# A hybrid state-space and attention layer with another work sequence, another share for GpSimd, and p's first tokens loaded by themselves

## The chip, the core and the metric

The kernel runs on one core of one Trainium2 chip. The core has a matrix engine (TensorE, PE in the profile, with its weight loads as PEld), a vector engine (VectorE, DVE), an engine for activations (ScalarE, ACT), a general engine (GpSimd, POOL) and SyncE (SP), which issues the DMAs of this kernel. The engines work side by side, each through its own list of instructions, and wait for each other by semaphores. The metric is the device time of one execution in microseconds; the median of the runs counts.

## The reference

One layer for 1024 tokens of 1024 values. All is float32.

```python
x = layer_norm(x, ln_emb_g, ln_emb_b)
z = x @ w_in                                  # 1024 -> 1984
xs, gs, cq, ckv, kr, gm = split(z, 512, 512, 256, 128, 64, 512)
ys = s5_branch(xs, ...) * silu(gs)            # 32 groups of 16 channels, 64 complex states each,
                                              # linear recurrence over the tokens, GELU, sigmoid GLU
ym = mla_branch(cq, ckv, kr, ...) * silu(gm)  # 4 heads, RMS-normed latents, rotary part of 64,
                                              # causal softmax, 128 queries at a time
mix = concat(ys, ym) @ w_out                  # 1024 -> 1024
u = alpha * x + mix
out = layer_norm(u + sigmoid(u @ w_pg) * (p @ w_pp), ln_g, ln_b)
```

## The kernel before

**Precision.** A float32 product is made as three matmuls of a faster type: each operand is split into a high part (a cast) and a low part (a subtraction), and high·high, high·low and low·high are added up in PSUM (`mm3`, `split`). So each loaded weight tile costs one cast and one subtraction before TensorE may use it. In the names, an h or l at the end is the high or low part: wh and wl of a tile of w_in, yTh and yTl of an S5 output, pth and ptl of transposed softmax weights.

**Stages.** First p @ w_pp (tile pp, with p's and w_pp's parts in pr, ph, pl), kept in DRAM until the end. At the same time x is normalised and transposed (xt, xh, xl). Then the projection z in tiles of 128 columns by 512 tokens: xs first (the S5 input), then gm, the latents ("lat": cq, ckv, kr, gathered in Z) and gs. Beside it runs the S5 branch in four blocks b of 8 groups: matrices ("mats": mo, mt, bbh, bbl, transposed through TensorE into wt, kt, kb), input, state and output (y, sy, hu). Then the latents are normalised and transposed (cqh, krh, krl), `fold` multiplies the two up-projections of the query into wf (wfh, wfl), and `q_nope` and `q_rope` make the queries (qn, qr). Attention runs over 16 items, each a head and a pair of query blocks, in four stages one item apart: `scores` (s, masked p, softmax with rrec as 1/sum), `probs_t` (pt is the transposed p, pth and ptl its parts), `pv` (o, oh, ol) and `uv_out` (uv, gated into ymt and ymh). The GLU of the S5 output reads yT back from DRAM (`glu_y`), multiplies the S5 gate gsr by yT (`glu_gs` loads, `glu_yg` multiplies), makes glu tiles of 12 matmuls, and a sigmoid sg whose product is ysh and ysl. Last come the output projection op, u, the gate g and the second normalisation.

**What sets the order.** No instruction is issued where it is written. The kernel calls a `Plan`, which records each operation with what it reads and writes (`record`). At the end `issue` goes over all of them: it keeps a time for each engine, takes the operation that can start soonest by its own estimates (`cost`, a model of TensorE's clock, and `ports`, since VectorE and GpSimd share access to SBUF), prefers the smaller "pri" where several can, and sends the resulting order to the engines. All instructions therefore bear line 441 in the profile; names tell them apart. Some operations have several ways ("AV", "VG"): any of the engines named may do them, and the plan takes the one that ends first by its estimate. Tiles of 128 by 1024 come from a pool of 40 buffers (u), of 128 by 512 from one of 12 (h), PSUM from two large and four small ones; a tile waits until a buffer of its pool is free.

**Tables.** "pri" is the place at which an operation is recorded plus a shift. MAIN is the sequence of the projection's own steps (gm, lat, gs tiles, loads `w_load`, splits `w_split`). After each gm, lat or gs tile and after each attention step, `after` raises a step counter and records from S5, LAT and GLU what is due at that step. SHIFT moves the priority of each of these streams, AHEAD that of single names in it, and S5_LATE stands in for S5's shift in the attention loop. ATTEND gives the order of the attention items.

```python
plan.shift = (S5_LATE if stream is S5 and late else shift) + AHEAD.get(name, 0)
work[name](*args)
```

**Start.** `warm` multiplies zeros (8 matmuls) while the first loads are under way. `pp_load` loads 512 tokens of p, or 512 columns of w_pp, for one of two halves k of the inner dimension; `pp_split` splits the same piece; `pp_tile(t, c)` makes 128 tokens by 512 columns.

Of the kernel before, what the change touches and what calls it, by code (L numbers as in the profile page):

```python
# [52 lines left out]
def _cw_parts(c, bits, n):  # L53
# [13 lines left out]
MAIN = [  # L67
    ("w_load", 11), ("w_split", 11), ("gm", 0, 0), ("gm", 0, 1), ("w_load", 10), ("w_split", 10), ("w_split", 9),
    ("gm", 1, 0), ("gm", 1, 1), ("wt_load",), ("gm", 2, 0), ("gm", 2, 1), ("gm", 3, 0), ("wt_split", 2),
    ("w_load", 4), ("wt_split", 0), ("wt_split", 1), ("wt_split", 3), ("lat", 0), ("gm", 3, 1), ("lat", 1),  # L70
    ("lat", 2), ("lat", 6), ("lat", 7), ("lat", 4), ("w_load", 5), ("lat", 3), ("lat", 5), ("w_load", 6),
    ("w_split", 5), ("gs", 1, 0), ("w_split", 4), ("w_load", 7), ("w_split", 6), ("w_split", 7), ("gs", 1, 1),
    ("gs", 0, 0), ("gs", 0, 1), ("gs", 2, 0), ("gs", 2, 1), ("gs", 3, 0), ("gs", 3, 1),
]


S5 = [
    (0, "mats", 0), (0, "in", 0), (0, "mats", 1), (0, "mats", 0), (0, "mats", 0), (0, "usplit", 0), (0, "state", 0),
    (3, "mats", 1), (4, "mats", 1), (4, "in", 1), (4, "usplit", 1), (6, "out", 0), (7, "mats", 2), (7, "state", 1),
    (7, "in", 2), (8, "out", 1), (8, "mats", 2), (9, "mats", 2), (9, "usplit", 2), (11, "phase", 1), (12, "state", 2),  # L80
    (12, "out", 2), (14, "mats", 3), (17, "in", 3), (17, "mats", 3), (20, "mats", 3), (24, "usplit", 3),
    (26, "state", 3), (32, "out", 3),
]
LAT = [
    (11, "lat_alloc"), (17, "lat_norm", 1), (18, "lat_transpose", 1), (18, "lat_norm", 0), (18, "mask"),
    (19, "lat_transpose", 0), (20, "fold"), (20, "q_rope", 0), (21, "q_rope", 1), (23, "q_rope_t", 0),
    (23, "q_nope", 0, 0), (24, "q_nope", 0, 1), (24, "q_rope_t", 1), (27, "q_nope", 1, 0), (27, "q_nope", 2, 0),
    (27, "q_nope", 1, 1), (28, "q_nope", 2, 1), (30, "q_nope", 3, 0), (30, "q_nope", 3, 1),
]
GLU = [  # L90
    (31, "glu_w"), (32, "glu_y", 2), (35, "glu_y", 1), (37, "glu_y", 0), (37, "glu_gs", 1), (37, "glu_yg", 1),
    (39, "glu_y", 3), (39, "glu_gs", 2), (39, "glu_yg", 2), (39, "glu_gs", 3), (39, "glu_yg", 3), (39, "wo_load", 1),
    (39, "glu", 1, 0), (40, "wo_load", 0), (40, "glu_gs", 0), (40, "glu_yg", 0), (40, "glu", 0, 0), (40, "glu", 0, 1),
    (41, "glu", 2, 0), (42, "wo_split", 0), (42, "glu", 3, 0), (42, "glu", 2, 1), (42, "glu", 1, 1),
    (42, "glu", 3, 1),
]
# [23 lines left out]
class Plan:  # L120
# [74 lines left out]
    def record(self, ways, args=()):  # L195
# [46 lines left out]
    def cost(eng, method, out, ins, kw):  # L242
# [202 lines left out]
def trunk(ctx, tc, I, out):  # L445
# [434 lines left out]
    def q_rope_t(hf):  # L880
        qd = L.pop(("qd", hf))
        for h in range(H):
            if hf == 0:
                qr[h] = U("qr", F32R)
            ps = PB("qrt", dt=F32R)
            for j in range(4):
                T.transpose(ps[:, j * P : j * P + P], qd[j][:, h].rearrange("p a b -> p (a b)"), identr)
            cpy(A if h % 2 else V, qr[h][:, hf * 512 : hf * 512 + 512], ps)

    def q_nope(h, hf):  # L890
# [541 lines left out]
    for k in range(2):  # L1432
# [197 lines left out]
```

## Time and profile before

| | |
|---|---|
| three timed runs | 587.05, 584.58, 587.03 us (median 587.03) |
| the profiled execution | 585.17 us, of which its span is 583.5 |
| granted clock of TensorE, mean | 0.995 |
| instructions | PE 2936, VectorE 968, ScalarE 517, GpSimd 100 |
| moved by DMA | 76.67 MB, 131 GB/s in the mean |

How to read it: a window row gives the busy time of each engine in a stretch of the span; a wait row names the engine, what it was about to write, and the engine and tile that ended the wait, with total, count and longest. In a timeline row stand the start, the duration, engine, operation, what is written and read, and, in brackets, the idle time just before with what ended it. "PEclk" is the share of full clock that TensorE was granted. A line without a time in front and with a bar is a group: busy total, mean in ns, idle before.

### The profile page before, as it was taken

The page shows a single profiled execution, that of the slowest core. Times are in us where ns is not written, and L with a number is a line of the kernel's source. Part 1 is how long each engine was busy: PE and PEld are TensorE (multiplying, and loading weights), DVE is VectorE, ACT ScalarE, POOL GpSimd, SP SyncE. Part 2 cuts the span into 40 slices and gives each one's busy share as a digit, 9 for nine tenths or more (in the row PEclk, how much of TensorE's full clock was granted, in tenths as well). Part 3 has the DMA queues.
Part 4 walks back from the last instruction along what each step waited for, and adds up shares of the span by engine and source line. Part 5 has one row for each costly group of instructions (what it writes and reads, how often), then busy time and mean ns, then how long its engine had stood idle before and what let it go on. Part 6 is the DMA issues. An engine that isn't in the chain of part 4 may idle for free.

```text
span 583.5 us, 8264 instructions
## 1 busy us (share of the span) xinstructions
PE 559.1 (96%) x2936; PEld 475.9 (82%) x2936; DVE 457.5 (78%) x968; ACT 272.8 (47%) x517; POOL 83.6 (14%) x100
## 2 busy tenths in 40 slices
PE   8989989999999999999999999799999999999994
PEld 7867878788898878878889998688888888888884
DVE  6999999989999987467998888968344337577666
ACT  5777136446282853256766876644111014123221
POOL 0000004202010144211722312001000001000000
PEclk9999989999999999999999999999999999999999
DMA  8898433532111332121004313716543567934301
GB/s 298 321 352 275 145 97 88 204 113 108 73 68 46 126 113 73 37 74 37 0 2 148 106 37 101 261 54 235 127 121 78 108 151 239 346 112 163 108 38 72
DMA packets 71577, 76.67 MB, mean 131 GB/s; under 512 B 37920, under 2 KB 52448, under 8 KB 71536
## 3 DMA queue, kind: packets, MB, share of 16 engines
q1 hardware_dynamic: 71536, 76.14, 40.1%
q8 instruction: 23, 0.38, 0.3%
q14 instruction: 18, 0.15, 0.1%
HBM read 50.47 MB, written 25.66 MB: 130 GB/s over the span
## 4 chain that ended last, share of the span: by engine, by line
PE 56%; DVE 5%; issue 1%; ACT 1%; DVEq 0%
PE g L441 15%; PE op L441 15%; PE s L441 6%; PE z L441 4%; PE o L441 4%; PE glu L441 3%; PE pt L441 2%; PE qn L441 2%; PE uv L441 1%; PE qrp L441 1%; DVE gsr L441 1%; PE y L441 1%; DVE p L441 1%; DVE hh L441 0%; PE qrt L441 0%
## 5 line engine op out<-in xcount | busy, mean ns | idle before, releaser
L441 PE MATMUL z<-xh,wh 128*128 128x512 f32 x192 | 76.2, 397 | 1.3 <-DVE krh L441 1.3
L441 PE MATMUL z<-xh,wl 128*128 128x512 f32 x192 | 75.5, 395 | 1.1 <-DVE wl L441 1.1
L441 PE MATMUL z<-xl,wh 128*128 128x512 f32 x192 | 76.1, 396 | 0.0
L441 PE MATMUL g<-wpl,uh 128*128 128x512 f32 (+1 forms) x136 | 51.2, 377 | 0.0
L441 PE MATMUL g<-wph,ul 128*128 128x512 f32 (+1 forms) x136 | 51.2, 376 | 0.0
L441 PE MATMUL g<-wph,uh 128*128 128x512 f32 (+1 forms) x136 | 51.2, 376 | 0.0
L441 PEld LDWEIGHTS z<-xh,wh 128*128 128x128 f32 x192 | 36.4, 190 | 8.5 <-DVE krh L441 1.5
L441 PEld LDWEIGHTS z<-xh,wl 128*128 128x128 f32 x192 | 36.4, 190 | 8.5 <-DVE wl L441 1.7
L441 PEld LDWEIGHTS z<-xl,wh 128*128 128x128 f32 x192 | 36.5, 190 | 6.9
L441 DVE SCALAR_TENSOR_TENSOR xr<-xr,op 128x512 f32<-128x512 f32 x16 | 11.0, 686 | 39.1 <-PE op L441 39.1
L441 ACT CAST uh<-xr 128x512 fp32r<-128x512 f32 x16 | 9.9, 621 | 64.8 <-DVE xr L441 51.5
L441 PEld LDWEIGHTS g<-wpl,uh 128*128 128x128 f32 x136 | 25.6, 188 | 4.8
L441 PEld LDWEIGHTS g<-wph,ul 128*128 128x128 f32 x136 | 25.6, 188 | 4.7
L441 PEld LDWEIGHTS g<-wph,uh 128*128 128x128 f32 x136 | 25.6, 188 | 4.6
L441 DVE CUSTOM_DVE_ANT_0 p<-s,mask 128x128 f32<-128x128 f32 (+7 forms) x32 | 23.8, 752 | 4.0 <-PE s L441 3.8
L441 DVE TENSOR_TENSOR ptl<-pt,pth 128x512 fp32r<-128x512 f32 (+3 forms) x48 | 25.3, 551 | 0.9 <-ACT pth L441 0.4
L441 ACT ACTIVATE p<-p,mx 128x128 f32<-128x128 f32 (+7 forms) x32 | 24.7, 773 | 2.7 <-DVE mx L441 2.6
L441 PE MATMUL op<-ysh,woh 128*128 128x512 f32 x64 | 24.9, 389 | 0.0
L441 PE MATMUL op<-ysl,woh 128*128 128x512 f32 x64 | 24.9, 389 | 0.0
L441 PE MATMUL op<-ysh,wol 128*128 128x512 f32 x64 | 24.9, 389 | 0.0
L441 PE MATMUL op<-ymh,woh 128*128 128x512 f32 x64 | 24.9, 389 | 0.0
L441 PE MATMUL op<-yml,woh 128*128 128x512 f32 x64 | 24.9, 389 | 0.0
(368 smaller groups left out, 1620.1 us busy)
## 6 DMA issues: line engine op xcount, KB each, us to landing
wr<-in_w_fm SPq DMA_DIRECT2D x12, 512.0 KB, 6.3
x<-in_x SPq DMA_DIRECT2D x8, 512.0 KB, 8.8
d_pp<-ppo SPq DMA_DIRECT2D x8, 512.0 KB, 4.8
d_xln<-xt SPq DMA_DIRECT2D x16, 256.0 KB, 6.2
wor<-in_w_out SPq DMA_DIRECT2D x8, 512.0 KB, 4.6
xr<-d_xln SPq DMA_DIRECT2D x8, 512.0 KB, 5.4
d_ut<-ut SPq DMA_DIRECT2D x64, 64.0 KB, 1.9
utok<-d_ut SPq DMA_DIRECT2D x16, 256.0 KB, 5.3
```

What stands on the lines that cost most here:

```text
L441: getattr(self.real[ran[i]], method)(*ops[i]["args"], **kw)
```

## The change

- MAIN, S5, LAT and GLU get other sequences and step numbers; SHIFT, AHEAD and S5_LATE get other numbers. So the same work is recorded at other places and with other priorities.
- A list NOT_G names tiles whose operations lose the choice of GpSimd: bbl, kd, mo, pl, uql, vvl. Names are compared whole, without the number; the tiles that the S5 matrices use are called kdl, so "kd" meets none of these.
- `cost`: a VectorE operation with an input in SBUF that is read with a stride is estimated at 0.07 + 1.95 per thousand elements, and a power on GpSimd at 0.35 + 210 per thousand. Estimates only: no instruction is changed by them, but the order and the engine can be.
- `pp_load` and `pp_split` take a part. For p's first half of the tokens, 128 tokens are loaded and split first, then the other 384: two DMAs, two casts and two subtractions more.
- `warm` issues 6 matmuls, not 8.
- Bookkeeping that the sequences need (assertions, an earlier place for Y), which issues nothing.

```diff
 MAIN = [
-    ("w_load", 11), ("w_split", 11), ("gm", 0, 0), ("gm", 0, 1), ("w_load", 10), ("w_split", 10), ("w_split", 9),
+    ("w_load", 11), ("w_split", 9), ("w_load", 10), ("gm", 0, 0), ("w_split", 11), ("gm", 0, 1), ("gm", 1, 0),
...
 GLU = [
-    (31, "glu_w"), (32, "glu_y", 2), (35, "glu_y", 1), (37, "glu_y", 0), (37, "glu_gs", 1), (37, "glu_yg", 1),
+    (30, "glu_y", 2), (31, "glu_w"), (33, "glu_y", 0), (34, "glu_gs", 1), (35, "glu_gs", 2), (36, "glu_y", 1),
...
-S5_LATE = -20
...
-SHIFT = [(S5, -2560), (LAT, -760), (GLU, -2090)]
+S5_LATE = 50
+
+NOT_G = ["bbl", "kd", "mo", "pl", "uql", "vvl"]
...
+SHIFT = [(S5, -3920), (LAT, -1380), (GLU, -1400)]
...
+        if len(ways) > 1 and outs[0].tensor.name.split("_")[0].rstrip("0123456789") in NOT_G:
+            ways = [w for w in ways if w[0] != "G"]
...
+            if any(a.space != PSUM and a.ap[-1][0] not in (0, 1) for a in ins):
+                return 0.07 + 1.95 * k
             return 0.07 + ptr + 1.045 * k
...
         if eng == "G":
+            if kw.get("op") == ALU.pow:
+                return 0.35 + 210 * k
...
-    def pp_load(v, n, k, c):
-        s = slice(c * 512, c * 512 + 512)
+    def pp_load(v, n, k, c, part=slice(0, 512)):
+        s = slice(c * 512 + part.start, c * 512 + part.stop)
         SY.dma_start(out=v[k][0][:, s], in_=I[n][k * P : k * P + P, s])
...
-    def pp_split(v, k, c):
-        s = slice(c * 512, c * 512 + 512)
+    def pp_split(v, k, c, part=slice(0, 512)):
+        s = slice(c * 512 + part.start, c * 512 + part.stop)
         r, h, l = v[k]
         split(h[:, s], l[:, s], r[:, s])
...
-        for _ in range(8):
+        for _ in range(6):
             mm(ps, z[:, 0:P], z[:, 0:512], True, True)
...
     warm()
+    first, then = slice(0, P), slice(P, 512)
     for k in range(2):
+        pp_load(ppt, "p_t", k, 0, first)
         pp_load(wpt, "w_pp", k, 0)
-        pp_load(ppt, "p_t", k, 0)
+    for k in range(2):
+        pp_load(ppt, "p_t", k, 0, then)
...
     for k in range(2):
+        pp_split(ppt, k, 0, first)
         pp_split(wpt, k, 0)
-        pp_split(ppt, k, 0)
+    for k in range(2):
+        pp_split(ppt, k, 0, then)
```

Three places where this moves instructions. The first is TensorE at the first transposes of an S5 matrix: z_327 is a projection tile, xh and xl its token side, wh_217 and wl_218 its weights, and wt is the transposed matrix made from bbh. Before:

```order
L441 MATMUL z_327<-xh_150,wh_217 128x512
L441 MATMUL z_327<-xl_151,wh_217 128x512
L441 MATMUL z_327<-xh_150,wl_218 128x512
L441 MATMUL z_327<-xh_154,wh_217 128x512
L441 MATMUL z_327<-xl_155,wh_217 128x512
L441 MATMUL z_327<-xh_154,wl_218 128x512
L441 MATMUL z_327<-xh_158,wh_217 128x512
L441 MATMUL z_327<-xl_159,wh_217 128x512
L441 MATMUL z_327<-xh_158,wl_218 128x512
L441 MATMUL wt_344<-ic_280,bbh_320 128x160 x3
L441 MATMUL wt_345<-ic_280,bbh_320 128x160 x3
```

After the change:

```order
L449 MATMUL z_327<-xh_150,wh_217 128x512
L449 MATMUL z_327<-xl_151,wh_217 128x512
L449 MATMUL z_327<-xh_150,wl_218 128x512
L449 MATMUL z_327<-xh_154,wh_217 128x512
L449 MATMUL wt_346<-ic_280,bbh_320 128x160 x3
L449 MATMUL wt_347<-ic_280,bbh_320 128x160 x3
L449 MATMUL z_327<-xl_155,wh_217 128x512
L449 MATMUL z_327<-xh_154,wl_218 128x512
L449 MATMUL z_327<-xh_158,wh_217 128x512
```

The wt rows stand behind four matmuls of the z tile where they stood behind nine; the other five follow them.

The second place is VectorE at the normalised latents: sy is a part of the S5 output, rv a small step of a norm (from the sum of squares ssq), wh and wl weights of later projections, Z the latents. Before:

```order
L441 TENSOR_TENSOR bbl_533<-mo_530,bbh_532 128x1024
L441 TENSOR_TENSOR sy_519<-y_522,yt_523 128x512
L441 TENSOR_SCALAR rv_557<-ssq_100 128x4 x2
L441 CAST wh_546<-wr_543 128x1024
L441 TENSOR_TENSOR wl_545<-wr_536,wh_544 128x1024
L441 TENSOR_TENSOR wl_547<-wr_543,wh_546 128x1024
L441 TENSOR_SCALAR Z_525<-Z_525,rms_500 128x256
```

After the change, ahead of the same step:

```order
L449 TENSOR_TENSOR sy_521<-y_522,yt_523 128x512
L449 TENSOR_TENSOR sy_521<-y_524,yt_525 128x512
L449 COPY kt_535<-wt_536 128x96
L449 TENSOR_TENSOR bbl_518<-mo_515,bbh_517 128x1024
L449 TENSOR_SCALAR rv_554<-ssq_100 128x4
L449 COPY kt_535<-wt_537 128x96
L449 TENSOR_SCALAR Z_476<-Z_476,rms_551 128x256
```

And further down, where two weight parts now are (krh and krl are the parts of the rotary key, ro and qro belong to the rotary queries):

```order
L449 COPY krh_548<-krt_599 128x512
L449 TENSOR_TENSOR kl_545<-ckt_598,kh_544 128x512
L449 COPY krl_549<-krt_600 128x512
L449 TENSOR_TENSOR wl_572<-wr_506,wh_571 128x1024
L449 TENSOR_TENSOR ro_607<-qrp_605,cos_98 128x256
L449 TENSOR_TENSOR ro_607<-qrp_605,sin_99 128x256
L449 TENSOR_TENSOR wl_574<-wr_530,wh_573 128x1024
```

One wh cast and two wl subtractions have left the stretch ahead of Z; the wl stand behind krl and the wh has gone to ScalarE. Two kt copies are in the stretch now; the bbl subtraction is there in both.

The third place is TensorE at the end of attention, with the last transposes pt of the softmax weights p, and glu tiles. Before:

```order
L441 MATMUL uv_1039<-oh_1015,wuv_596 128x256
L441 MATMUL uv_1039<-ol_1016,wuv_596 128x256
L441 MATMUL uv_1039<-oh_1015,wuvl_597 128x256
L441 MATMUL pt_1056<-ident_75,p_1020 128x128 x2
L441 MATMUL glu_1050<-yTh_1042,wgh_850 128x512
L441 MATMUL pt_1056<-ident_75,p_1020 128x128 x2
L441 MATMUL glu_1050<-yTl_1043,wgh_850 128x512
L441 MATMUL glu_1050<-yTh_1042,wgl_851 128x512
L441 MATMUL pt_1057<-ident_75,p_1020 128x128 x3
L441 MATMUL pt_1058<-ident_75,p_1025 128x128 x4
L441 MATMUL pt_1059<-ident_75,p_1025 128x128 x4
L441 MATMUL o_1060<-pth_1029,vh_495 128x256
```

After the change:

```order
L449 MATMUL glu_1069<-yTh_829,wgh_858 128x512
L449 MATMUL glu_1069<-yTl_830,wgh_858 128x512
L449 MATMUL glu_1069<-yTh_829,wgl_859 128x512
L449 MATMUL glu_1069<-yTh_1044,wgh_858 128x512
L449 MATMUL glu_1069<-yTl_1045,wgh_858 128x512
L449 MATMUL glu_1069<-yTh_1044,wgl_859 128x512
L449 MATMUL pt_1075<-ident_75,p_1022 128x128 x4
L449 MATMUL pt_1076<-ident_75,p_1022 128x128 x3
L449 MATMUL pt_1077<-ident_75,p_1027 128x128 x4
L449 MATMUL pt_1078<-ident_75,p_1027 128x128 x4
L449 MATMUL o_1079<-pth_1031,vh_546 128x256
```

The transposes stood between matmuls of a first GLU tile, glu_1050; now glu_1069, the seventh of these tiles, ends ahead of them.

More of the change, by code (lines that the diff above doesn't have):

```diff
@@ L67 @@
 MAIN = [
-    ("w_load", 11), ("w_split", 11), ("gm", 0, 0), ("gm", 0, 1), ("w_load", 10), ("w_split", 10), ("w_split", 9),
[L69 to L72, printed above, removed]
@@ L73 @@
-    ("gs", 0, 0), ("gs", 0, 1), ("gs", 2, 0), ("gs", 2, 1), ("gs", 3, 0), ("gs", 3, 1),
+    ("w_load", 11), ("w_split", 9), ("w_load", 10), ("gm", 0, 0), ("w_split", 11), ("gm", 0, 1), ("gm", 1, 0),
+    ("w_split", 10), ("wt_load",), ("gm", 1, 1), ("gm", 2, 0), ("wt_split", 1), ("gm", 2, 1), ("wt_split", 3),
+    ("wt_split", 0), ("gm", 3, 0), ("gm", 3, 1), ("wt_split", 2), ("lat", 2), ("lat", 0), ("lat", 3), ("lat", 4),
+    ("w_load", 4), ("w_load", 7), ("w_split", 4), ("w_load", 5), ("lat", 5), ("lat", 6), ("lat", 1), ("w_split", 5),
@@ L74 @@
+    ("lat", 7), ("w_load", 6), ("gs", 1, 0), ("gs", 0, 0), ("w_split", 7), ("w_split", 6), ("gs", 1, 1), ("gs", 0, 1),
+    ("gs", 2, 0), ("gs", 2, 1), ("gs", 3, 0), ("gs", 3, 1),
 ]
 S5 = [
-    (0, "mats", 0), (0, "in", 0), (0, "mats", 1), (0, "mats", 0), (0, "mats", 0), (0, "usplit", 0), (0, "state", 0),
-    (3, "mats", 1), (4, "mats", 1), (4, "in", 1), (4, "usplit", 1), (6, "out", 0), (7, "mats", 2), (7, "state", 1),
-    (7, "in", 2), (8, "out", 1), (8, "mats", 2), (9, "mats", 2), (9, "usplit", 2), (11, "phase", 1), (12, "state", 2),
@@ L81 @@
-    (12, "out", 2), (14, "mats", 3), (17, "in", 3), (17, "mats", 3), (20, "mats", 3), (24, "usplit", 3),
-    (26, "state", 3), (32, "out", 3),
+    (0, "in", 0), (0, "mats", 0), (0, "mats", 0), (0, "usplit", 0), (0, "mats", 1), (0, "state", 0), (1, "mats", 1),
+    (1, "in", 1), (2, "out", 0), (3, "mats", 1), (4, "mats", 0), (5, "usplit", 1), (6, "in", 2), (6, "mats", 2),
+    (7, "state", 1), (7, "out", 1), (7, "mats", 2), (10, "mats", 2), (11, "phase", 1), (11, "usplit", 2),
+    (11, "in", 3), (11, "state", 2), (13, "mats", 3), (14, "out", 2), (16, "mats", 3), (21, "mats", 3),
@@ L83 @@
+    (23, "usplit", 3), (26, "state", 3), (30, "out", 3),
 ]
 LAT = [
[L85 to L88, printed above, removed]
+    (16, "lat_alloc"), (17, "lat_norm", 1), (17, "lat_transpose", 1), (17, "lat_norm", 0), (19, "fold"),
@@ L89 @@
+    (20, "lat_transpose", 0), (20, "q_rope", 1), (20, "q_rope", 0), (21, "mask"), (23, "q_nope", 0, 0),
+    (23, "q_rope_t", 0), (23, "q_rope_t", 1), (24, "q_nope", 0, 1), (27, "q_nope", 1, 0), (27, "q_nope", 2, 0),
+    (27, "q_nope", 1, 1), (27, "q_nope", 2, 1), (27, "q_nope", 3, 0), (27, "q_nope", 3, 1),
 ]
 GLU = [
-    (31, "glu_w"), (32, "glu_y", 2), (35, "glu_y", 1), (37, "glu_y", 0), (37, "glu_gs", 1), (37, "glu_yg", 1),
-    (39, "glu_y", 3), (39, "glu_gs", 2), (39, "glu_yg", 2), (39, "glu_gs", 3), (39, "glu_yg", 3), (39, "wo_load", 1),
@@ L93 @@
-    (39, "glu", 1, 0), (40, "wo_load", 0), (40, "glu_gs", 0), (40, "glu_yg", 0), (40, "glu", 0, 0), (40, "glu", 0, 1),
-    (41, "glu", 2, 0), (42, "wo_split", 0), (42, "glu", 3, 0), (42, "glu", 2, 1), (42, "glu", 1, 1),
-    (42, "glu", 3, 1),
+    (30, "glu_y", 2), (31, "glu_w"), (33, "glu_y", 0), (34, "glu_gs", 1), (35, "glu_gs", 2), (36, "glu_y", 1),
+    (37, "glu_yg", 2), (38, "glu_yg", 1), (38, "glu_gs", 3), (39, "glu_y", 3), (39, "glu", 1, 0), (39, "wo_load", 1),
+    (39, "glu_gs", 0), (39, "glu_yg", 0), (39, "glu", 0, 0), (39, "glu", 0, 1), (39, "glu_yg", 3), (39, "glu", 2, 0),
@@ L96 @@
+    (39, "glu", 3, 0), (39, "glu", 2, 1), (39, "glu", 1, 1), (41, "glu", 3, 1), (41, "wo_load", 0),
+    (42, "wo_split", 0),
 ]
@@ L101 @@
 ]
-S5_LATE = -20
-AHEAD = {"fold": 200, "glu": -930, "glu_gs": -110, "glu_w": -60, "glu_y": 300, "in": 400, "lat_alloc": -500, "lat_norm": -160, "lat_transpose": -1100, "mask": -400, "mats": -170, "out": 30, "phase": -300, "q_nope": 30, "q_rope": 500, "q_rope_t": 200, "state": -400, "usplit": 30, "wo_load": 30, "wo_split": -30}
-SHIFT = [(S5, -2560), (LAT, -760), (GLU, -2090)]
+S5_LATE = 50
+NOT_G = ["bbl", "kd", "mo", "pl", "uql", "vvl"]
+AHEAD = {"fold": 700, "glu": -1400, "glu_gs": 690, "glu_w": 670, "glu_y": -30, "glu_yg": -410, "in": 160, "lat_alloc": -440, "lat_norm": -890, "lat_transpose": -1800, "mask": -470, "mats": 200, "out": 300, "phase": -830, "q_nope": -1100, "q_rope": 600, "q_rope_t": 510, "state": -370, "usplit": -100, "wo_load": -560, "wo_split": 620}
+SHIFT = [(S5, -3920), (LAT, -1380), (GLU, -1400)]
 class _Engine:
@@ L755, in trunk @@
     gs = {}
+    Y = {}
     def gs_tile(m, hf):
@@ L763, in gs_tile @@
             SY.dma_start(out=d_gs[m], in_=gs[m])
+            Y[m, "gs"] = True
     gmt = {}
@@ L888, in q_rope_t @@
             cpy(A if h % 2 else V, qr[h][:, hf * 512 : hf * 512 + 512], ps)
+        L["qr", hf] = True
     def q_nope(h, hf):
@@ L898, in q_nope @@
         hi, lo = qn[h]
+        L["qn", h, hf] = True
         act(hi[:, ss], ps, AF.Copy, scale=kvg)
@@ L914, in scores @@
     def scores(h, qb):
+        assert ("qr", qb // 4) in L and ("qn", h, qb // 4) in L
         n = (qb + 1) * P
@@ L1244, in s5_out @@
         M[b, "out"] = True
-    Y = {}
     ysT = {}
@@ L1268, in glu_gs @@
     def glu_gs(m):
+        assert (m, "gs") in Y
         g = Y["gs", m] = U("gsr")
@@ L1274, in glu_yg @@
         mul(g, g, Y[m][0].rearrange("p (j n) -> p n j", j=CT))
+        Y[m, "yg"] = True
     def glu(m, hf):
@@ L1280, in glu @@
             ysT[m] = U("ysh", F32R), U("ysl", F32R)
+        assert (m, "yg") in Y
         ps = PB("glu")
```

## The prediction

> **What bounds the kernel now.** First the page: busy shares, then the chain that ended last.
>
> ```profile
> PE 559.1 (96%) x2936; PEld 475.9 (82%) x2936; DVE 457.5 (78%) x968; ACT 272.8 (47%) x517; POOL 83.6 (14%) x100
> ...
> PE 56%; DVE 5%; issue 1%; ACT 1%; DVEq 0%
> ```
>
> TensorE (PE) is busy for 96% of the 583.5 us span and is most of the chain. Its work stays as it is (the diff takes two warm-up matmuls away), so only its idle time and its half-speed time can be won. Where these lie, the windows show: stretch, length, then the busy time of PE, PEld, DVE, ACT and POOL, the granted clock, the DMA share, GB/s.
>
> ```profile
> core 0: us, PE busy (x) PEld busy (x) DVE busy (x) ACT busy (x) POOL busy (x), PEclk, DMA share, GB/s
> 60.00:82.00 22.00, 20.32 (x90) 16.50 (x88) 22.00 (x102) 4.69 (x9) 0.00 (x0) 1.00 0.41 131
> ...
> 86.00:190.00 104.00, 102.56 (x540) 89.02 (x539) 100.65 (x169) 52.23 (x114) 17.65 (x17) 1.00 0.29 98
> 190.00:260.00 70.00, 68.30 (x376) 56.73 (x374) 53.32 (x103) 36.29 (x77) 19.70 (x21) 1.00 0.24 81
> 260.00:350.00 90.00, 88.48 (x605) 80.70 (x606) 77.59 (x214) 65.01 (x139) 27.79 (x32) 1.00 0.18 59
> 350.00:380.00 30.00, 25.21 (x160) 21.71 (x159) 26.08 (x50) 18.50 (x37) 4.90 (x6) 1.00 0.50 177
> ...
> 400.00:575.00 175.00, 175.00 (x797) 145.91 (x796) 104.01 (x164) 41.64 (x60) 7.38 (x9) 1.00 0.52 153
> ```
>
> Three regimes. Up to about 190 us VectorE (DVE) is full (22.00 of 22.00, 100.65 of 104.00): it sets the pace, and whatever PE gains ahead of it is lost again at the next wait for VectorE. From 190 to 350 VectorE has air (53.32 of 70.00) and PE loses little. From 350 to 380 PE is idle for 4.79 us, the largest loss in one place. From 400 to 575 PE has no gap: 175.00 of 175.00. A gain before that stretch reaches the end undiminished; the stretch itself offers nothing. Then the waits of PE, with total, count and longest:
>
> ```profile
> PE pt L441 <- ACT sg L441: 2.2, 1, 2.2
> ...
> PE wt L441 <- ACT bbh L441: 2.0, 1, 2.0
> ...
> PE z L441 <- DVE krh L441: 1.3, 1, 1.3
> PE z L441 <- DVE wl L441: 1.1, 1, 1.1
> ...
> PE qn L441 <- DVE wfl L441: 0.8, 1, 0.8
> PE y L441 <- DVE tl L441: 0.7, 2, 0.4
> ...
> PE cqt L441 <- DVE Z L441: 0.2, 1, 0.2
> ```
>
> **The change part by part.** The sum is made against the profiled execution: 585.17 us, a span of 583.5 and 1.67 around it. The three timed runs lie 0.59 below it and 1.88 and 1.86 above, so on average 1.05 above.
>
> **Start (p in two parts, six warm-up matmuls).**
>
> ```profile
> 5.08 0.79 PE L441 MATMUL pp<-ph,ph 128*128 128x512 f32 x1
> 5.67 0.63 PE L441 MATMUL pp<-pl,ph 128*128 128x512 f32 x1
> 6.10 0.63 PE L441 MATMUL pp<-ph,ph 128*128 128x512 f32 x1
> ...
> 4.41 0.62 ACT L441 CAST ph<-pr 128x512 fp32r<-128x512 f32 x1 [0.46 <-DMA pr<-in_p_t]
> ```
>
> The first pp matmul waits for p's cast (4.41 + 0.62 = 5.03, it starts at 5.08). With a quarter of p first it can start up to 0.5 us earlier (the cast waited 0.46 for p to land), but now all six matmuls of a tile stand together, so PE waits for the second half of w_pp instead of working on other tiles. Two more DMAs on SyncE, two more casts on ScalarE and two more subtractions on VectorE come at no cost: ScalarE waits for landings there. Bounds: 0.5 earlier; at worst eight matmuls more at the slow pace of this place (6.10 − 5.67 = 0.43 against 0.23 at full clock), 8 × 0.2 = 1.6 later. I take 0, as VectorE decides the next 180 us and either end moves only PE. Without that cover it would be the 1.6.
>
> [...]
>
> **First wait for a state matrix (bbh).**
>
> ```profile
> 79.93 1.22 DVE L441 TENSOR_TENSOR mo<-mo,mt 128x1024 f32<-128x1024 f32 x1
> 81.19 1.04 ACT L441 CAST bbh<-mo 128x1024 fp32r<-128x1024 f32 x1 [2.28 <-DVE mo L441]
> 82.29 1.53 PE L441 MATMUL wt<-ic,bbh 128*128 128x160 f32 x6 [1.97 <-ACT bbh L441]
> ...
> 82.67:86.09 3.42, 3.42 (x13) 2.91 (x13) 3.42 (x5) 2.27 (x5) 0.00 (x0) 0.55 0.00 0
> ```
>
> mo on VectorE, bbh on ScalarE, then wt: one chain, set by VectorE. By my count of the instructions ahead of this mo, with the durations of their groups, VectorE has 75.3 us of work there before and after, so bbh comes at the same time. But nine z matmuls stood ahead of wt and now four do: the five others come behind it. The wait gets 5 × 0.227 = 1.13 longer (1.97 to 3.1). Behind the wt rows only z rows of the same tile queue, which VectorE does not need at once. The window behind the wait ran at 0.55 of the clock, about 3.42 × 0.45 = 1.5 lost, and stays so.
>
> **The rest of the front, to about 193 us.** VectorE decides here: my count to the last wait of this regime (y for hu) gives it 180.3 us before and 180.4 after. So PE's extra 1.13 is taken out of the smaller waits that follow (tl's 0.7 among them), and the wait for wl at 40 us (1.1), if it goes, comes back at bbh. Term: 0. Bounds from moving work between VectorE and GpSimd:
>
> ```profile
> 108.00 1.47 DVE L441 TENSOR_TENSOR rt<-im,es 128x512 f32<-128x512 f32 x1
> ...
> 107.64 1.28 POOL L441 TENSOR_TENSOR rt<-re,ec 128x512 f32<-128x512 f32 x1 [5.21 <-ACT wtl L441]
> ...
> 572.47 0.69 DVE L441 TENSOR_TENSOR ppr<-sgg,utok 128x512 f32<-128x512 f32 x1
> ```
>
> VectorE's rt took 1.47 beside a GpSimd rt; an operation of that size with two SBUF inputs takes 0.69 where GpSimd is idle (the ppr row). It began 0.36 after the other and ended after it: VectorE was held for some 0.8. GpSimd gains three large subtractions here (tl, wl, a second wtl) and loses mo and mt, which is a net of one: with 0.8 to 2 us per collision, 0 to +2. On the other side, if VectorE's smaller load (it loses some 1.6 us in all) lies in the front, −1.5.
>
> [...]
>
> **Latents, keys and fold, 190 to 262 us.**
>
> ```profile
> L441 DVE TENSOR_TENSOR wl<-wr,wh 128x1024 fp32r<-128x1024 f32 x12 | 14.7, 1240 | 0.0
> ...
> L441 DVE CAST wh<-wr 128x1024 fp32r<-128x1024 f32 x3 | 2.1, 686 | 0.0
> ...
> 219.75 0.50 PE L441 MATMUL z<-xh,wh 128*128 128x512 f32 x1 [1.27 <-DVE krh L441]
> ...
> 260.80 0.50 PE L441 MATMUL qn<-cqh,wfl 128*128 128x512 f32 x1 [0.82 <-DVE wfl L441]
> ```
>
> Ahead of the normalised latents Z, and so of krh, VectorE worked on one wh and two wl of later projections. Now these stand behind krl (the wh on ScalarE): 0.69 + 2 × 1.24 = 3.2 us less in front. That is more than the wait of 1.27, with VectorE loaded to 53.32 of 70.00, so it goes. fold, which makes wfl, is issued far earlier and its 0.82 goes. With Z's 0.2 that is 2.3. What is late next is a projection behind the moved wl: I put 0.3 there. Term: −2.0; ends −4 (PE's pace loss beside these stops goes too) and 0 (wl late for what they are worth).
>
> **End of attention and GLU, 350 to 380 us.**
>
> ```profile
> 358.91 0.30 PE L441 MATMUL pt<-ident,p 128*128 128x128 f32 x1 [1.11 <-DVE ol L441]
> ...
> 370.39 0.40 PE L441 MATMUL glu<-yTh,wgl 128*128 128x512 f32 x1
> 373.04 0.55 PE L441 MATMUL pt<-ident,p 128*128 128x128 f32 x3 [2.25 <-ACT sg L441]
> 374.08 1.09 PE L441 MATMUL pt<-ident,p 128*128 128x128 f32 x8 [0.49 <-DVE ol L441]
> 375.61 0.39 PE L441 MATMUL o<-pth,vh 128*128 128x256 f32 x1 [0.43 <-DVE ptl L441]
> 376.85 0.50 PE L441 MATMUL glu<-yTh,wgh 128*128 128x512 f32 x1 [0.51 <-DVE ptl L441]
> ...
> 369.92 3.77 DVE L441 TENSOR_TENSOR gsr<-gsr,yT 128x1024 f32<-128x1024 f32 x2
> L441 DVE TENSOR_TENSOR yTl<-yT,yTh 128x1024 fp32r<-128x1024 f32 x4 | 4.9, 1220 | 0.0
> ```
>
> The last transposes pt need PSUM that sg, ol and the ptl give back, and VectorE is in two gsr products for 3.77 us just then, with the ol behind them. The five waits sum to 4.79. Now seven GLU tiles stand ahead of these transposes, of 12 matmuls each; 64 of them directly ahead, 64 × 0.227 = 14.5 us of work that needs neither p nor ol. That covers the 3.77 on VectorE. What takes its place: a gsr and a yTl, 3.77 / 2 + 1.22 = 3.1 us together, now stand ahead of a 1/sum of softmax amid attention (I put 0.8), and the last o, uv and the last GLU tile follow each other with nothing between (0.5). Term: −4.79 + 1.3 = −3.5; ends −4.8 and 0.
>
> **The cost of stopping.** From 370.39 to 373.04 are 2.65 us, of which the pace takes 0.23: the stop cost 2.42, not 2.25. Five stops that go at some 0.1 each: −0.5, ends −1 and 0.
>
> The corrected estimates cost nothing by themselves; they only set the order. **Sum:** 0 + 0 − 2.0 − 3.5 − 0.5 = −6.0, so 579.2 in the profiled execution, and 1.05 above that for a median of runs: **580.2 us**.
>
> **The rivals.** *New waits for old.* For it speaks that VectorE's total falls by under 2 us, so what is moved out of one place is late in another. The attention part would give nothing, the latent part half (−1), and a collision in the front takes 0.5 back: 585.17 − 1 + 0.5 + 1.05 = 585.7. Against it: VectorE has air from 190 on, and the GLU block covers by plain row order. That the change doesn't do what it says belongs here: "kd" in the list fits no tile (the tile is kdl), so those subtractions stay on GpSimd; they cost no PE wait before, so nothing changes by it.
>
> *More than counted.* Everything that can be won behind 190 goes (−4, −4.8, −1), and VectorE's front is 1 to 2 us shorter: 585.17 − 9.8 − 1.5 + 1.05 = 574.9. For it: PE's losses there are all waits for VectorE. Against it: a full VectorE to 190 must get shorter by itself.
>
> *Slower: softmax rows wait for a buffer.* yT and gsr, now asked for earlier on SyncE, sit in the same 40 buffers as p, pth and ptl of attention.
>
> ```profile
> L441 DVE CUSTOM_DVE_ANT_0 p<-s,mask 128x128 f32<-128x128 f32 (+7 forms) x32 | 23.8, 752 | 4.0 <-PE s L441 3.8
> ```
>
> The 32 masked rows p waited for the scores (3.8 of 4.0), so no buffer was short before. If each waited 0.4 us for one, 32 × 0.4 = 12.8 and the time is 593; it turns slower than before by over 0.5% from (590.0 − 580.2) / 32 = 0.31 us a row.
>
> **How the numbers follow.** Forecast 0.58 (about 577 to 583.5), new waits for old 0.18, more than counted 0.15, slower 0.09. A measurement of this kernel tells some 0.5% from no change: below 584.1 is faster (0.58 + 0.15 = 0.73), above 590.0 slower (0.09), between them same (0.18). For 8 in 10 the range takes in the forecast, most of the larger gain and most of the first rival: 574.5 to 586.
>
> **What would show it.** In the new profile: a wait for bbh of about 3 us with the clock near half behind it; no wait for krh or wfl over 0.5; PE idle for 1 to 2 us in the stretch that holds the last transposes, and GLU matmuls without a gap ahead of them; VectorE still full up to about 190 us. Wrong would be: a wait for a new name of over 2 us behind 190, p rows that wait for anything but s, or y for hu later than 193 us by over 2.

## The result, and the profile after

| | before | after |
|---|---|---|
| median of the runs | 585.26 us (6 runs) | 581.38 us (6 runs; 581.19 without the one of 1422) |
| profiled execution, its span | 585.17, 583.5 | 582.14, 580.4 |
| ratio after to before, 95% interval | | 0.9923 (0.9906 to 0.9939) |
| the same kernel again (e5 below) | | 0.9911 (0.9890 to 0.9932) |

By the two ratios the kernel is 4.5 and 5.2 us faster (0.8 and 0.9%), by the medians 4.1 and 5.1, where 6.0 was forecast. One execution of the kernel after took 1422 us and the profiled one of e11 below 1118; both are left out of every comparison.

First the page of the kernel after, engines and chain:

```profile
PE 558.5 (96%) x2934; PEld 475.5 (82%) x2934; DVE 455.3 (78%) x973; ACT 275.8 (48%) x516; POOL 90.1 (16%) x100
...
PE 72%; DVE 18%; ACT 3%; DMA 3%; issue 2%; SPq 1%; POOL 0%; DVEq 0%; POOLq 0%
```

The shares tell nothing of the gain. DVE's part of the chain has grown from 5% to 18%, and that is a first hint of where some of it was lost. The windows of the kernel after, columns as before:

```profile
0.00:60.00 60.00, 52.58 (x247) 41.57 (x248) 50.49 (x136) 39.97 (x62) 3.39 (x13) 1.00 0.84 306
60.00:86.00 26.00, 23.07 (x101) 19.04 (x100) 25.97 (x111) 7.40 (x16) 0.00 (x0) 0.94 0.43 137
86.00:190.00 104.00, 101.89 (x523) 86.73 (x523) 95.85 (x161) 51.29 (x112) 15.90 (x17) 0.98 0.31 101
190.00:260.00 70.00, 69.87 (x386) 60.04 (x385) 60.80 (x115) 36.36 (x73) 25.75 (x23) 1.00 0.22 73
260.00:350.00 90.00, 89.25 (x607) 80.73 (x606) 76.84 (x210) 66.14 (x138) 26.52 (x26) 1.00 0.20 65
350.00:380.00 30.00, 30.00 (x184) 26.77 (x183) 27.26 (x57) 21.30 (x41) 7.15 (x8) 1.00 0.36 123
380.00:400.00 20.00, 19.53 (x115) 17.12 (x114) 13.00 (x21) 11.30 (x19) 2.04 (x2) 1.00 0.39 135
```

and the two windows of the front for the kernel before that were not shown:

```profile
0.00:60.00 60.00, 55.05 (x257) 44.54 (x258) 51.90 (x137) 41.45 (x62) 3.39 (x13) 1.00 0.89 314
60.00:86.00 26.00, 24.03 (x102) 19.75 (x101) 26.00 (x107) 7.19 (x14) 0.00 (x0) 0.93 0.35 111
```

Subtract TensorE's busy time from each length. From 190 to 400 us it idled 1.70 + 1.52 + 4.79 + 0 = 8.0 us before and 0.13 + 0.75 + 0 + 0.47 = 1.35 after: 6.7 us won, a little more than forecast. From 0 to 190 it idled 4.95 + 1.97 + 1.44 = 8.4 before and 7.42 + 2.93 + 2.11 = 12.5 after: 4.1 lost, where 0 was forecast (2.3 lost in the second profile of the same kernel, e5, by the same subtraction).

Windows cut the work at fixed times. An instruction cuts it better: the y matmul on hu that the prediction put at 193 us, the end of the front. TensorE has about the same work before it in both kernels (902 matmuls before, 906 after, without the warm-up). In TensorE's timelines it stands at

```profile
193.31 0.39 PE L441 MATMUL y<-hu,vvh 128*128 128x256 f32 x1 [0.17 <-DVE hu L441]
```

```profile
199.16 0.28 PE L449 MATMUL y<-hu,vvh 128*128 128x256 f32 x1
```

before and after, and at 196.70 in e5. From there to the end the kernel takes 390.2 us before, 381.2 after and 381.3 in e5. Four matmuls, 0.9 us at the 0.227 of the prediction, only changed sides. Without them about 8 us were won behind the front, more than the 6.0 forecast, and 2.5 to 5 were lost in it. (This mark also counts matmuls that run more slowly, which idle time does not.)

VectorE shows why the front lost: in 86 to 190 it was busy for 100.65 of 104 and is now busy for 95.85. It waits there. Its waits up to 200 us in the kernel after (the kernel before had suu 0.4 and ph 0.2, and neither kt nor this wl):

```profile
DVE suu L449 <- ACT suu L449: 2.9, 2, 2.3
DVE kt L449 <- ACT wth L449: 1.6, 1, 1.6
DVE ph L449 <- ACT es L449: 1.1, 1, 1.1
...
DVE wl L449 <- DMA d_pp<-ppo: 0.9, 1, 0.9
```

And TensorE's waits in the kernel after. Those on sg, ol, krh, wl and wfl are gone, the one on bbh has grown:

```profile
PE xt L449 <- DVE xt L449: 4.2, 3, 1.9
PE wt L449 <- ACT bbh L449: 2.9, 1, 2.9
...
PE wt L449 <- DVE im L449: 1.0, 1, 1.0
...
PE o L449 <- DVE ptl L449: 0.5, 1, 0.5
```

### The profile page after: what moved, and what is told of

Same layout as the page of the kernel before. It is cut to its first block, busy times and chain, and to the rows that moved or that the text cites. A ratio compares the mean times of both kernels' runs of the same rounds, so it can differ in the third digit from the quotient of the medians.

```text
span 580.4 us, 8272 instructions
## 1 busy us (share of the span) xinstructions
PE 558.5 (96%) x2934; PEld 475.5 (82%) x2934; DVE 455.3 (78%) x973; ACT 275.8 (48%) x516; POOL 90.1 (16%) x100
## 4 chain that ended last, share of the span: by engine, by line
PE 72%; DVE 18%; ACT 3%; DMA 3%; issue 2%; SPq 1%; POOL 0%; DVEq 0%; POOLq 0%
PE g L449 15%; PE op L449 15%; PE z L449 12%; PE s L449 6%; PE o L449 5%; PE zl L449 4%; PE glu L449 4%; PE y L449 2%; PE pt L449 2%; PE qn L449 2%; DVE bn L449 2%; DMA d_pp<-ppo 1%; DVE rt L449 1%; PE uv L449 1%; DVE p L449 1%
## 5 line engine op out<-in xcount | busy, mean ns | idle before, releaser
L449 ACT ACTIVATE sgg<-g 128x512 f32<-128x512 f32 (+1 forms) x17 | 9.6, 565 | 36.9 <-PE g L449 36.9
L449 POOL TENSOR_TENSOR yml<-ymt,ymh 128x256 fp32r<-128x256 f32 x16 | 16.6, 1041 | 62.8 <-ACT ymh L449 56.7
```

What stands on the lines that cost most here:

```text
L449: getattr(self.real[ran[i]], method)(*ops[i]["args"], **kw)
```

## The experiments

Most experiments leave the recording and the plan as they are, so that every engine gets the order of the kernel after, and move single operations in the finished list (a change of the recording would let the plan reorder far more):

```diff
-            for _, _, i in sorted(order):
+            seq = [i for _, _, i in sorted(order)]
+
+            def ahead(ids, mark):
+                for i in ids:
+                    seq.remove(i)
+                at = seq.index(mark)
+                seq[at:at] = ids
+
+            ...
+            for i in seq:
```

**The start.** e1 puts the start of before back: whole halves of p, eight warm-up matmuls, before's order of the first pp matmuls. e9 does the same with six warm-up matmuls, and e10 has nothing but eight.

```diff
+            for i in (11, 13, 35, 36, 39, 40):
+                seq.remove(i)
+            ahead([12, 15, 14, 16], 17)
+            ahead([37, 38, 43, 44, 41, 45, 42, 46], 47)
...
+            seq[seq.index(10):seq.index(10)] = [10, 10]
```

(11 to 16 are the loads, 35 to 46 the splits, of which 15, 16 and 43 to 46 take the whole half; the lines left out order the pp matmuls; 10 is a warm-up matmul. e9 lacks the last line, e10 has only it.)

> The kernel after with the start of before (p in whole halves, eight warm-up matmuls, before's order of the first 18 pp matmuls); everything else keeps the order of after. Theory A (VectorE sets the pace of the front, and the two extra loads hold up its LayerNorm statistics by 0.65 us): statistics start at 10.5 instead of 11.1 us, and the sum of the first state matrix (mo, first of 128x1024 with mt) ends 0.6 to 1.6 us earlier; the time falls by 0.6 to 1.6 us against after's 581.4. Rival B (the start is hidden, as the prediction had it): within 0.3 us of 581.4, and the first mo sum at the same time as in after.

> The kernel after with p loaded and split in whole halves as before, and before's order of the first pp matmuls, but still six warm-up matmuls. Theory A (the loads hold VectorE up: in the runs so far its first LayerNorm statistic began at 10.5, 9.8, 10.1 and 10.5 us with the loads of before and at 11.1, 10.8, 10.9, 11.6, 11.6 and 12.3 with those of the change): statistics at 9.8 to 10.5 us, time as e1, 1 to 1.5 us below after (about 579). Rival B (the two warm-up matmuls matter, by a clock that opens later): time 0.5 us or more above e1's ratio of 0.9897, with pp matmuls 0.43 us apart beyond 7.6 us.

> The kernel after with eight warm-up matmuls instead of six, nothing else. Theory A: statistics at 10.8 to 12.3 us as in after, time within 0.5 us of after (ratio 0.991 to 0.9925). Rival B: the time falls by 0.5 us or more (ratio 0.990 or less), since TensorE's clock opens earlier.

Measured: e1 0.9897 (0.9877 to 0.9916), e9 0.9872 (0.9854 to 0.9891), e10 0.9916 (0.9895 to 0.9937). So with whole loads the time is 1 to 3 us below the kernel after; the intervals of e9 and e10 don't overlap. The warm-up matmuls by themselves are worth nothing that can be measured. VectorE's timelines around its first LayerNorm statistic (bn), of before, after and e1 in this order:

```profile
9.78 0.69 DVE L441 TENSOR_TENSOR pl<-pr,ph 128x512 fp32r<-128x512 f32 x1 [0.19 <-ACT ph L441]
10.48 1.29 DVE L441 BATCH_NORM_STATS2 bn<-x 128x6 f32<-128x512 f32 x2
```

```profile
10.50 0.69 DVE L449 TENSOR_TENSOR pl<-pr,ph 128x512 fp32r<-128x512 f32 x1 [0.81 <-ACT ph L449]
11.13 1.29 DVE L449 BATCH_NORM_STATS2 bn<-x 128x6 f32<-128x512 f32 x2
```

```profile
8.31 1.47 DVE L466 TENSOR_TENSOR pl<-pr,ph 128x512 fp32r<-128x512 f32 x2 [0.52 <-ACT ph L466]
9.80 1.29 DVE L466 BATCH_NORM_STATS2 bn<-x 128x6 f32<-128x512 f32 x2
```

The statistics stand right behind the last pl of w_pp, which waits for its cast (0.81 us in the kernel after, 0.19 before), and that for its load (0.88 and 0.27). One profile would not show it, since two executions of the kernel after already differ (that pl began at 10.50 us, and at 10.19 in e5); over all of them it is plain. With whole loads the first statistic began at 10.48, 10.07, 9.80, 10.49, 9.75 and 9.81 us (before, e7, e1, e8, e9, e12; mean 10.1), with split loads at 11.13, 10.87, 11.55, 11.56, 10.79, 12.34 and 10.83 (after, e5, e2, e3, e4, e6, e10; mean 11.3). In the first 9 us the core's DMAs moved 225 GB/s before and 242 in e9, but 200 after and 176 in e2. Whether the smaller loads or their order cause this was not tried. The windows 0 to 9 of after and e9:

```profile
0.00:9.00 9.00, 6.76 (x18) 3.88 (x19) 3.59 (x11) 5.51 (x9) 1.05 (x11) 1.00 0.66 200
```

```profile
0.00:9.00 9.00, 6.38 (x14) 4.60 (x15) 3.87 (x9) 5.96 (x8) 1.04 (x11) 1.00 0.76 242
```

VectorE's late start is passed on in full: from the first statistic to the first wt matmul it is 71.8 us before and 71.7 to 72.8 in the profiles of all other runs but e11. TensorE's start is hidden for the most part only. In e9 the first pp matmul started at 5.55 and the slow pace (0.43 us a matmul) lasted to about 9.5 us; from 30 us on VectorE waited three times for a cast xh, 1.6 us in all, against twice and 1.1 us in e1, and the stretch to wt took 72.8 us against 71.7 in e1.

Not all of the 1 to 3 us is the start, either. In the profiles of e1 and e9 no half-clock stretch follows the wait for bbh (the z matmuls behind it stand 0.23 us apart), while one does in after and e5 (0.43 apart; next part), and the mean granted clock was 0.997 in all four executions of e9, against 0.989 to 0.997 in the kernel after. What the profiles show of the start by itself is the 1.2 us of the statistic.

**The z matmuls and the suu cast.** e2 puts the five z matmuls (729 to 733) back ahead of the first wt (801). e3 puts ScalarE's two suu casts (842, 844) ahead of its copy of xs (749), and leaves wt where the change has it.

```diff
+            ahead([729, 730, 731, 732, 733], 801)
```

```diff
+            ahead([842, 844], 749)
```

> The kernel after with the five z matmuls put back ahead of the first wt transposes, nothing else moved. Theory A (the delayed z tile holds ScalarE's xs copy, the suu cast queued behind it and VectorE's suu): PE's wait for bbh falls from 2.9 to about 1.8 us, VectorE's wait for suu from 2.3 to about 1.2 or less, and the time by about 1.1 us (580.3). Rival B (VectorE's chain to bbh sets the end, PE has slack behind it): wait for bbh 1.8, but the wait for suu and the time as in after (581.4).

> The kernel after with ScalarE's two suu casts put ahead of its xs copy, nothing else moved. Theory A (VectorE waits 2.3 us for suu only because the cast stands behind a copy that waits for a late z tile): VectorE's wait for suu falls below 0.5 us, and the time by 1.5 to 2.3 us (about 579.5). Rival B (VectorE would wait just behind it for the next thing, for instance for wt tiles or the second bbh): the wait for suu goes, other waits of VectorE between 90 and 120 us grow by as much, time within 0.5 of 581.4.

Measured: e2 0.9897 (0.9881 to 0.9913), e3 0.9902 (0.9884 to 0.9920), about 1 us below the kernel after each; the intervals overlap with those of the kernel after, and e3 stays below the 1.5 to 2.3 us that theory A gave it. TensorE's wait for bbh is 1.8 us in e2, as expected, and 2.9 in e3. In both VectorE's long wait for suu is gone (0.5 in all), and in e3 no other wait of VectorE has grown by it. The chain in the kernel after, from its timelines (TensorE, then ScalarE, then VectorE):

```profile
83.85 1.57 PE L449 MATMUL wt<-ic,bbh 128*128 128x160 f32 x6 [2.93 <-ACT bbh L449]
...
89.57 0.55 PE L449 MATMUL z<-xh,wl 128*128 128x512 f32 x1
...
92.21 0.59 ACT L449 COPY xs<-z 128x512 f32<-128x512 f32 x1 [3.96 <-PE z L449]
92.70 0.62 ACT L449 CAST suu<-su 128x512 fp32r<-128x512 f32 x1
...
93.35 0.69 DVE L449 TENSOR_TENSOR suu<-su,suu 128x512 fp32r<-128x512 f32 x1 [2.34 <-ACT suu L449]
```

The z tile ends late, since five of its matmuls stand behind the wait and run at half clock (0.43 apart until 89.57). ScalarE waits for that tile in order to copy xs, and the suu cast, whose data has long been there, waits behind the copy. VectorE's next instruction is the suu subtraction, and it waits.

But the delay isn't always there. In e1 and e9 the wait for bbh was 2.9 as well and VectorE waited only 0.5 for suu, because no half-clock stretch followed (with 3.4 us of it, in e5, the wait was 1.1). TensorE's timeline in e1:

```profile
81.54 0.90 PE L466 MATMUL wt<-ic,bbh 128*128 128x160 f32 x6 [2.91 <-ACT bbh L466]
```

Six wt matmuls took 0.90 there and 1.57 in the kernel after. So the moved wt costs where the clock drops behind it, and about nothing where it doesn't. The price can be read off: from the first wt matmul to this suu subtraction VectorE needs 7.08 us in e1 and e9, 8.3 in e4, e5 and e10 (3.4 us at half clock) and 9.5 in the kernel after (5.7). That is 1.2 and 2.4 us. With the casts moved it is 7.08 in e3 too, although 3.4 us of half clock follow the wait there; this is what shows the mechanism. e2 can't show it, since no half-clock stretch followed its wait.

**The GLU block.** e4 is the kernel after with the GLU table, the GLU shift and the GLU and wo priorities of before; e7 is the kernel before with those of the change. Both are planned anew, and in both the order is unchanged up to about 300 us.

```diff
-    (30, "glu_y", 2), (31, "glu_w"), (33, "glu_y", 0), (34, "glu_gs", 1), (35, "glu_gs", 2), (36, "glu_y", 1),
+    (31, "glu_w"), (32, "glu_y", 2), (35, "glu_y", 1), (37, "glu_y", 0), (37, "glu_gs", 1), (37, "glu_yg", 1),
...
-SHIFT = [(S5, -3920), (LAT, -1380), (GLU, -1400)]
+SHIFT = [(S5, -3920), (LAT, -1380), (GLU, -2090)]
```

> The kernel after with the GLU table, the GLU shift and the GLU and wo priorities of before; the order is the same as in after up to about 300 us. Theory A (the GLU block ahead of the last transposes is what removed the stops of the attention's end): TensorE idle 4 to 5 us again between 345 and 390 us, time 585 to 586, about that of the kernel before. Rival B (attention's end was relieved by the latent part, which runs ahead): idle below 2 us there, time below 583.

> The kernel before with the GLU table, the GLU shift and the GLU and wo priorities of the change, and nothing else of it; its order is that of before up to about 300 us. Theory A (the GLU part by itself takes the stops out of the end of attention): TensorE idle below 1.5 us between 350 and 392 us, time 4 us below before (about 581). Rival B (it needs the latent part, which brings the attention forward, or it makes new waits in attention): idle above 2.5 us, time above 583.

Measured: e4 0.9994 (0.9980 to 1.0008): without the GLU part all of the gain is gone, 4 to 5 us, and the stops are back. TensorE's waits of e4, and its window:

```profile
PE pt L449 <- ACT sg L449: 2.1, 1, 2.1
...
PE pt L449 <- DVE ol L449: 1.5, 2, 1.2
```

```profile
350.00:380.00 30.00, 26.35 (x152) 22.67 (x151) 24.48 (x47) 17.70 (x35) 6.17 (x7) 0.89 0.46 170
```

TensorE idles for 3.65 us there, somewhat less than the 4 to 5 expected, but its clock is at 0.89 where the kernel before had 1.00. So a part of the 4 to 5 us is clock.

e7 0.9972 (0.9961 to 0.9984): alone it brings 1.6 us, not 4. TensorE's idle time between 350 and 392 us is 1.39, as theory A had it, but the time is that of the rival. The stops at 370 us are gone, and new ones stand earlier in attention, at 323 and 358 us. TensorE's waits of e7, and VectorE's timeline at the second of them:

```profile
PE pt L441 <- ACT p L441: 1.0, 1, 1.0
PE s L441 <- DVE mx L441: 1.0, 1, 1.0
```

```profile
353.69 2.04 DVE L441 TENSOR_TENSOR gsr<-gsr,yT 128x1024 f32<-128x1024 f32 x1
355.64 1.78 DVE L441 TENSOR_TENSOR yTl<-yT,yTh 128x1024 fp32r<-128x1024 f32 x1
357.34 0.14 DVE L441 TENSOR_SCALAR mx<-mx 128x1 f32<-128x1 f32 x1
```

The work that left the end of attention now stands in front of a row maximum. In the kernel after the same kind of block sits ahead of a 1/sum (the 0.8 us that the prediction set aside), and TensorE doesn't wait there (30.00 of 30.00 from 350 to 380). Nor does it wait as e7 does at 323 us: the stretch 300 to 350 has 0.2 us of TensorE idle in after and e5 against 1.8 in e7. Which of the other parts of the change gives it this room was not tried by itself.

**The latents.** e6 puts VectorE work back ahead of Z: nine multiplications that nobody reads.

```diff
+            seq[at.index(1754):at.index(1754)] = self.extra[1:] * 9
```

(1754 is the first scaling of Z; extra holds a memset and the multiplication of a spare tile of 128x224.)

> The kernel after with nine more VectorE multiplications of 128x224 (on a tile nobody reads, about 0.38 us each, 3.4 us together) put ahead of the first scaling of Z, that is as much work as the change has taken out of that place; all else as in after. Theory A (krh and wfl were waited for because that work stood in front): a wait of PE on krh or another latent tile of 1 to 2 us comes back between 205 and 262 us and the time rises by 1.3 to 2.5 us. Rival B (the earlier fold and the other order of projections had removed these waits by themselves): no wait over 0.5 us there, time within 0.5 us of the kernel after.

Measured: 0.9979 (0.9958 to 0.9999), 3 to 4 us above the kernel after, more than expected. TensorE's timeline in e6:

```profile
212.50 0.44 PE L455 MATMUL cqt<-ident,Z 128*128 128x128 f32 x2 [2.68 <-DVE Z L455]
...
215.85 0.63 PE L455 MATMUL z<-xl,wh 128*128 128x512 f32 x1
216.28 0.55 PE L455 MATMUL z<-xh,wl 128*128 128x512 f32 x1
```

Of 3.5 us added 2.7 come out as a wait, on Z itself and not on krh, and behind it z matmuls are again 0.43 apart until about 216.3. So VectorE has less than a microsecond in hand at this place, and its work ahead of Z sets when TensorE goes on. The price is not that of the kernel before, though: there 3.2 us more work in front cost TensorE 1.6 us of idle time, and here 3.5 us cost 2.7 and some half clock, as the order around Z is another.

**Mending the front.** e5 is the kernel after once more. e11 lets VectorE do three rt and re operations (878, 881, 879) ahead of the kt copy (952) for which it waited 1.6 us. e8 has e1, e2, e3 and e11 together, e12 has e9, e2 and e3.

```diff
+            ahead([878, 881, 879], 952)
```

> The kernel after itself, unchanged in order, beside the others of this group. Both theories: 580.5 to 582 (ratio to before 0.991 to 0.994). It also shows how long the half-clock stretch behind the wait for bbh is in another execution: after's profile had 5.7 us, the first four experiments 0, 0, 3.4 and 3.4 us with waits of 2.9, 1.8, 2.9 and 2.9.

> The kernel after with VectorE's three first rt and re operations ahead of the kt copy for which it waited 1.6 us, nothing else. Theory A (VectorE sets the pace there): wait for kt below 1.0 us or gone, time 0.6 to 1.6 us below after (ratio 0.989 to 0.990). Rival B (the scan's first input comes from GpSimd at the same time anyway): VectorE waits for rt instead, time within 0.4 us of after.

> The kernel after with the start of before, the five z matmuls back ahead of wt, ScalarE's two suu casts ahead of the xs copy, and VectorE's three first rt and re operations ahead of the kt copy that waited 1.6 us. Theory A (VectorE's delays in the front add up): about 1.5 below after for the start, 1.3 for z and suu together, 0.5 to 1.5 for kt, so 577 to 578. Rival B (what is won in the front is lost at the next wait, as two or three of these edits undo the same delay): 579 to 580.

> The kernel after with whole loads of p but six warm-up matmuls (as e9), the five z matmuls ahead of wt, and ScalarE's suu casts ahead of the xs copy; VectorE's kt copy where the change has it. If the kt copy is worth nothing (e11) and the warm-up matmuls are worth nothing (e10), the ratio is that of e8, 0.9843 within 0.002. If kt's 1.6 us counted once the other delays are gone, it is 0.986 or more.

Measured: e5 0.9911 (0.9890 to 0.9932), e11 0.9918 (0.9899 to 0.9938), e8 0.9843 (0.9823 to 0.9863), e12 0.9873 (0.9852 to 0.9894). e8, at 576.82 us, beats both kernels: 8 to 9 us below before, 3 to 5 below after. Its window and VectorE's wait for kt:

```profile
86.00:190.00 104.00, 102.23 (x535) 88.19 (x534) 99.68 (x169) 51.57 (x113) 15.43 (x17) 0.99 0.30 98
...
DVE kt L469 <- PE wt L469: 1.0, 1, 1.0
```

VectorE is at 99.68 of 104 again, against 95.85 after. e12, however, is at e9's level (0.9872): on top of the whole loads, the z matmuls and the suu casts brought nothing, as one expects where no half-clock stretch follows the wait (there was none in either profile).

What sets e8 apart from e12 is kt and two warm-up matmuls. The forecast for e12 put a ratio of 0.986 or more to kt, and 0.9873 falls there; the intervals of e8 and e12 overlap barely. The profiles help here. From VectorE's first suu subtraction to the y matmul at the end of the front, e12 and then e8:

```profile
89.16 0.69 DVE L467 TENSOR_TENSOR suu<-su,suu 128x512 fp32r<-128x512 f32 x1
...
194.94 0.28 PE L467 MATMUL y<-hu,vvh 128*128 128x256 f32 x1
```

```profile
89.31 0.69 DVE L469 TENSOR_TENSOR suu<-su,suu 128x512 fp32r<-128x512 f32 x1
...
194.25 0.28 PE L469 MATMUL y<-hu,vvh 128*128 128x256 f32 x1
```

That is 105.78 us in e12 and 104.94 in e8. In the kernel after, e1, e3, e5 and e9, which all leave kt in its place, it is 105.8. So the wait of 1.6 us at the kt copy costs 0.8 us, by one profile of e8, and e11, whose interval is 1.1 us wide to each side, could not tell that from nothing. What VectorE waited for in kt's place in e11 was not seen. With the three delays mended e8 reaches the end of the front at 194.25, 0.9 us behind the kernel before, about the work that changed sides.

## Why the prediction was right, point by point

- **What bounds the kernel.** Right: VectorE up to 190 us, and behind it single waits. The gain lies where it was put (6.7 us of idle time behind 190), and the losses lie in the front: VectorE starts later and waits more. One sign named for being right did not come: VectorE is not full up to 190 us (95.85 of 104). And one named for being wrong did: y for hu at 199.16 or 196.70, more than 2 behind 193.
- **Start, taken as 0 between −0.5 and +1.6.** Here a size was off, and it is the step that failed. It said that VectorE "decides the next 180 us and either end moves only PE". VectorE itself starts behind these loads: its first statistic came 1.2 us later in the mean (10.1 to 11.3), and that delay goes on to wt undiminished. The measured 1.2 lies inside the bounds, but by luck: the upper end, 1.6, stood for TensorE's slow pace, and not for a late VectorE. TensorE did start earlier (4.35 against 5.08), which won nothing. Two warm-up matmuls by themselves are worth nothing that was measured (e10). That six of them make the slow pace last eight matmuls longer was the author's estimate, and no run shows it: in the kernel after the pp matmuls stand 0.23 to 0.34 us apart from 7.23 us on, in the kernel before 0.23 from 8.04 on. In e9, with six and whole loads, the pace of 0.43 lasted to about 9.5 us, and the stretch from the statistic to wt took 1.1 us longer than in e1, with eight; what decided this was not tried.
- **bbh.** The wait grew as worked out, to 2.9 where 3.1 was said. That nothing needs the z tile at once was wrong: ScalarE's xs copy does, and VectorE's suu stands behind it (e3). The cost depends on the clock: 1.2 or 2.4 us of VectorE with a half-clock stretch (e5, after), nothing without (e1, e9). That the slow stretch "stays so" held in some executions only.
- **The rest of the front, taken as 0.** VectorE's load was counted rightly; its waits were not counted at all. kt (a wait of 1.6, which cost 0.8) is a round from VectorE over TensorE and ScalarE back, which an equal sum of work can't show. The wait for es (1.1) and, in the profile of after alone, the one of wl for a transfer (0.9) were not tried. GpSimd's share was not tried by itself either; e8 has it too, and its front loses nothing. That VectorE is held beside GpSimd stands in other rows too: suu took 1.42 us beside GpSimd's suu (131.91, before) and mo 2.91 beside its wtl (132.52, after), against 0.69 and 1.22 alone, while two ptl, which read PSUM, took 1.28 together beside its rt (279.84, before), as alone. The two cost some 0.7 and 1.7 us, about the 0.8 to 2 per collision of the prediction; that one made the front longer was not shown.
- **Latents, −2.0.** Right: idle from 190 to 260 us fell from 1.70 to 0.13, and the waits for krh and wfl are gone. e6 shows from the other side that VectorE's work ahead of Z counts; the share of the earlier fold was not tried by itself.
- **End of attention, −3.5.** Right, and somewhat low: from 4.79 to 0.47 idle (350 to 400 us), by the GLU tiles ahead of pt (e4). That the moved products could make waits inside attention was said at 0.8; in the kernel after it is less, in e7 it is more.
- **The sum.** −6.0 forecast, −4.5 and −5.2 measured. Two errors went against each other: behind the front about 8 us were won where 6.0 were counted, and the front, taken as 0, lost 2.5 to 5 by the late statistic, suu with the clock, kt and, in the profile of after, the wait for wl. So the mechanism behind 190 us was right, and that the sum came so close is in part luck. The loss is a part of the rival "new waits for old", but in another place than it named. "Slower" did not show: no p row waited for a buffer.

## What to carry to other kernels

An engine that is full is delayed by what stands at the head of its queue, and not only by the sum of its work: after adding up its load, follow each queue that it waits for (here a load, 1.2 us in the mean, and a cast behind an unrelated copy, 1.2 or 2.4). The first landing that the busiest engine needs is part of its chain: loading something else a little earlier came with those 1.2 us here. And when the same block of work can go to two places, test it in both kernels: the GLU part was worth 4 to 5 us taken from the new kernel, and 1.6 us added to the old one.

## What of the hardware was not expected

The same wait for bbh, 2.9 us, was followed by 5.7 us of half-clock matmuls (0.43 us apart, against 0.23) in the kernel after (wt at 83.85, the last slow z at 89.57), by some 3.4 us in e3, e4, e5 and e10, by some 6 in e6, and by none in e1 and e9; a wait of 1.8 us gave none in e2 and e12 and some 3.4 us in e8, and one of 2.0 us came ahead of such a stretch in the kernel before. The length of the wait doesn't decide it. The granted clock was 0.50 from 82.36 to 85.77 us in the kernel before (3.41 us), and from 83.05 to 89.87 in the kernel after (6.82 us), where the drop falls within the wait (80.92 to 83.85). What sets off such a stretch and what ends it, no run shows. Behind bbh it held VectorE up for 1.2 or 2.4 us here, which is as much as single parts of this change are worth; a reading of one profile for an effect of that size needs the medians beside it.
